# Fillers ahead of the first projection, an earlier load and narrower attention levels in a two-layer decoder trunk

## The chip, the cores and the metric

The kernel runs on one core of a Trainium2 chip. TensorE (PE) multiplies, VectorE (DVE) and ScalarE (ACT) do the elementwise work, GpSimd (POOL) does a few small operations and issues accumulating DMAs, SyncE (SP) issues the other DMAs. The metric is the device time of one execution in microseconds (us); lower is better.

## The reference

A hybrid decoder trunk of two layers over 512 positions and 1024 channels, in float32. Layer 0 mixes with an RG-LRU recurrence, layer 1 with gated linear attention; each mixer is followed by a convolutional gated FFN. Every sub-layer has an RMSNorm before and after, and adaLN gives shift, scale and gate from a conditioning vector `c`.

```python
c_act = jax.nn.silu(c)
for i in range(DEPTH):
    mod = (c_act @ ada_w[i] + ada_b[i])[:, None, :]
    sh_m, sc_m, gt_m, sh_f, sc_f, gt_f = jnp.split(mod, 6, axis=-1)
    h = rmsnorm(x, norm_g[i, 0]) * (1.0 + sc_m) + sh_m
    y = rglru_mixer(h, ...) if i % 2 == 0 else gla_mixer(h, ...)
    x = x + gt_m * rmsnorm(y, norm_g[i, 1])
    h = rmsnorm(x, norm_g[i, 2]) * (1.0 + sc_f) + sh_f
    x = x + gt_f * rmsnorm(conv_ffn(h, ...), norm_g[i, 3])
```

The first thing that TensorE has to project is `h @ rg_w_in` of layer 0, and `h` needs the row norms of `x` and the shift and scale of layer 0, so `c_act @ ada_w`. In the attention of layer 1 a chunk's decay products are formed level by level over blocks of 1, 2, 4 to 64 positions.

## The kernel before

Everything is transposed: channels lie on the 128 partitions (eight tiles `k`), positions on the 512 columns. Weights come in units of 128x1024 float32 (`unit`, loaded by `load_upto` on SP's queue into `raw`), are rounded to a single-pass type (fp32r) on ACT (`w`'s high half), and the rest is formed on DVE (low half) or, for some units, by an accumulating DMA of POOL (`accum`). Each product is three single-pass products: high x high, low activation x high, high x low weight (`mm3`). Matrix products of plain float32 need more passes; in the profile one of them leaves two records.

The kernel's operations are recorded first and then ordered by a planner (`Sched.order`, lines 190 to 344) that simulates the engines: TensorE's and SP's operations have the order of their recording as priority, and one that is not ready by the planner's clock is passed by later ones; DVE, ACT and POOL take the longest remaining chain first. The order that comes out is fixed on each engine. The planner adds 1.5 us to an accumulating DMA's end (line 325). Its clocks set the order only. On the chip each engine waits for semaphores in this order. Since helpers record every operation, all TensorE products carry line 455, DVE's lines 384, 397 and 408, ACT's 431 and 436.

The stretch that the change touches most stands at lines 519 to 671 and 882 to 913:

- SP loads `c` (`crow`), four pairs of `x`, parameters, the identity, and then row by row `adaT` tiles (`ada`) and weight units.
- TensorE spreads `c` over the partitions with two products of one row by 512 columns (`pc`), ACT applies silu to them (`cact`).
- ACT squares the eight tiles of `x`, DVE adds them in the groups of `SQ_GROUPS`. TensorE sums each group over the partitions with four 128x1 products (`nr0`), with fillers ahead of the groups by `WARM`: one four-pass product of `ones` and `x[0]` ahead of the first and of the second.
- `rstd_from` scales the sums on ACT (`sm`), raises them to -1/2 on POOL (`pow`) and spreads them with four 128x128 products (`rb0`).
- For each `k`, `ada_col` multiplies a 128x1024 tile of `adaT` by `cact` and sums the rows on DVE (once for scale, part 1; once for shift, part 0), ACT turns the sums into a column of `mod`. `h_tile` makes `t2` on DVE, the high half `hh` on ACT and the low half `hl` on DVE. Then TensorE adds 24 products into the eight accumulators `xps`. The tile `k = 0` goes in two halves of 256 columns (`FH`).

Behind it `conv4` reads the accumulators: ACT starts each with one tap, DVE adds three more (the "taps", `g<-mm,const,g`); they free the PSUM banks that the next projections (`gproj`) need. In the attention, `level_mm` multiplies, for each level `hb` and each of four blocks, up to 128 stationary columns with 64 moving ones, and `masked` copies the part that counts:

```python
        rows = P - hb
        rows = rows if rows <= 96 else P
        e.mms([(ps[t * n:(t + 1) * n].rows(rows), xt[t * P:t * P + rows], part3(xt[tsl(t)], 2 * hb, hb, 2 * hb),
```

## Time and profile before

| | us |
|---|---|
| median of 3 runs | 1181.31 |
| the runs | 1181.24, 1181.31, 1183.03 |
| the profiled execution | 1182.17 |
| its span, first to last instruction | 1180.40 |
| TensorE busy in it | 1167.3 |
| DVE, ACT, POOL busy | 839.4, 558.8, 45.5 |

Busy TensorE is modelled: matmuls are pipelined and the end of one lies behind the start of the next, so a busy share does not tell how fast products follow each other. For that, count how many start in a stretch. The granted clock is the share of full speed that the chip's record of the clock shows for a stretch; where there is no record, as ahead of the first change, the column shows 1.00. "Idle before" in brackets is the time for which an engine stood still before an instruction, and what ended it.

### The profile page before, as it was taken

Reading aid. Unit: us, or ns where it says so; the run is one execution under the profiler, and the core shown is the slowest. Engines: PE = TensorE matmul, PEld = TensorE weight load, DVE = VectorE, ACT = ScalarE, POOL = GpSimd, SP = SyncE. Lnnn points to the kernel's source line nnn. Section 1 sums busy time; section 2 is a strip of 40 time slices with the busy share of each in tenths; the row PEclk is TensorE's granted clock in tenths of the full one; section 3 lists DMA queues with packets and bytes.
Section 4 is the critical chain, followed back from the end, with each engine's and each line's share of the span. In section 5 each row is a group of like instructions: output and inputs, shape, how many; then the busy total and the mean of one; then the engine's idle time right before and its main releaser. Section 6 shows DMA issues by size and latency. Waiting matters only on the chain.

```text
span 1180.4 us, 16718 instructions
## 1 busy us (share of the span) xinstructions
PE 1167.3 (99%) x6556; PEld 1015.8 (86%) x6556; DVE 839.4 (71%) x1392; ACT 558.8 (47%) x882; POOL 45.5 (4%) x59
## 2 busy tenths in 40 slices
PE   8999999999999999999999999999999999999998
PEld 6876799988888888899988888999988888888897
DVE  5899978977778888568769576758745655645644
ACT  4489867643423424444478344445543333324421
POOL 0100014000000000000000000000000000000000
PEclk9999999999999999999999999999999999999999
DMA  9688589476574676221413102213142322232202
GB/s 348 246 260 268 177 263 286 163 231 218 171 221 176 204 237 202 89 92 55 141 63 107 55 24 84 72 40 105 42 156 90 107 101 96 91 106 90 72 1 72
DMA packets 48304, 165.81 MB, mean 140 GB/s; under 512 B 5249, under 2 KB 7809, under 8 KB 48226
## 3 DMA queue, kind: packets, MB, share of 16 engines
q1 hardware_dynamic: 45058, 156.36, 38.9%
q0 software_dynamic: 3168, 8.39, 3.8%
q8 instruction: 51, 0.84, 0.3%
q14 instruction: 27, 0.22, 0.1%
HBM read 162.63 MB, written 2.10 MB: 140 GB/s over the span
## 4 chain that ended last, share of the span: by engine, by line
PE 92%; ACT 3%; DVE 2%; issue 1%; DMA 1%; POOL 1%; DVEq 0%; POOLq 0%; ACTq 0%
PE mm L455 89%; PE nr L455 3%; ACT g L431 1%; DMA raw<-in_wall_dram 1%; POOL sm L388 1%; ACT w L436 1%; DVE gh L384 1%; ACT L431 1%; DVE g L384 0%; DVE gh L397 0%; DVE w L384 0%; DVE const L384 0%; ACT w L431 0%; DMA araw<-in_c_dram 0%; DVE araw L397 0%
## 5 line engine op out<-in xcount | busy, mean ns | idle before, releaser
L455 PE MATMUL mm<-g,w 128*128 128x512 f32 (+2 forms) x5069 | 949.8, 348 | 1.8 <-ACT g L431 1.3
L455 PEld LDWEIGHTS mm<-g,w 128*128 128x128 f32 (+1 forms) x5069 | 816.9, 189 | 121.9 <-ACT g L431 2.3
L436 ACT CAST w<-raw 128x1024 fp32r<-128x1024 f32 x178 | 186.0, 1046 | 213.7 <-PE mm L455 202.7
L384 DVE TENSOR_TENSOR w<-raw,w 128x1024 fp32r<-128x1024 f32 (+1 forms) x168 | 203.6, 1216 | 84.8 <-ACT w L436 83.9
L397 DVE SCALAR_TENSOR_TENSOR g<-mm,const,g 128x510 f32<-128x510 f32 (+3 forms) x205 | 151.0, 747 | 106.7 <-ACT g L431 96.2
L384 DVE TENSOR_TENSOR g<-g,g 128x512 f32<-128x512 f32 (+2 forms) x199 | 117.7, 613 | 35.0 <-ACT g L431 27.0
L431 ACT ACTIVATE g<-mm,const 128x512 f32<-128x512 f32 (+1 forms) x147 | 101.4, 696 | 18.6 <-PE mm L455 18.6
L455 PE MATMUL mm<-g,g 128*128 128x256 f32 (+4 forms) x748 | 103.1, 293 | 0.0
L431 ACT ACTIVATE g<-g 128x512 f32<-128x512 f32 (+1 forms) x132 | 66.5, 539 | 74.4 <-DVE g L397 65.9
L455 PEld LDWEIGHTS mm<-g,g 128*128 128x128 f32 (+1 forms) x748 | 95.2, 191 | 4.2
L397 DVE SCALAR_TENSOR_TENSOR araw<-araw,const 128x1024 f32<-128x1024 f32 x72 | 86.5, 1220 | 4.7 <-DMA araw<-in_adaT_dram 4.6
L436 ACT CAST g<-g 128x512 fp32r<-128x512 f32 (+1 forms) x63 | 39.1, 623 | 104.1 <-DVE g L384 103.2
L384 DVE TENSOR_TENSOR g<-g,mm 128x512 f32<-128x512 f32 (+1 forms) x80 | 45.2, 579 | 41.2 <-PE mm L455 40.6
L384 DVE TENSOR_TENSOR gh<-gh,gh 128x256 f32<-128x256 f32 x97 | 40.8, 422 | 25.3 <-ACT gh L431 23.4
L388 POOL TENSOR_TENSOR sm<-sm,const 128x2 f32<-128x2 f32 (+1 forms) x19 | 20.4, 1073 | 917.0 <-DVE sm L408 901.0
L455 PE MATMUL mm<-w,g 128*128 128x512 f32 x192 | 46.2, 394 | 0.0
L455 PEld LDWEIGHTS mm<-w,g 128*128 128x128 f32 x192 | 35.4, 188 | 7.0
L431 ACT ACTIVATE gh<-g 128x256 f32<-128x256 f32 x32 | 13.1, 416 | 54.8 <-DVE g L384 54.8
L431 ACT ACTIVATE g<-gh,const 128x256 fp32r<-128x256 f32 x50 | 23.6, 504 | 24.1 <-DVE gh L397 23.5
L436 ACT COPY g<-mm 128x512 f32<-128x512 f32 (+1 forms) x36 | 19.7, 560 | 24.6 <-PE mm L455 24.6
L397 DVE SCALAR_TENSOR_TENSOR w<-w,const 128x1024 f32<-128x1024 f32 x24 | 28.9, 1220 | 1.0 <-DMA w<-in_adaT_dram 1.0
L431 ACT ACT_TABLE_LOAD x22 | 28.2, 1283 | 1.1 <-PEq L1312 0.7
(72 smaller groups left out, 536.9 us busy)
## 6 DMA issues: line engine op xcount, KB each, us to landing
raw<-in_wall_dram SPq DMA_DIRECT2D x192, 512.0 KB, 3.6
araw<-in_adaT_dram SPq DMA_DIRECT2D x72, 512.0 KB, 4.5
w<-in_adaT_dram SPq DMA_DIRECT2D x24, 512.0 KB, 8.4
w<-in_wall_dram POOLq DMA_DIRECT2D x10, 512.0 KB, 8.5
g<-in_wall_dram POOLq DMA_DIRECT2D x12, 256.0 KB, 9.8
const<-in_xT_dram SPq DMA_DIRECT2D x4, 512.0 KB, 5.4
out_dram<-const SPq DMA_DIRECT2D x8, 256.0 KB, 2.3
araw<-in_masks_dram SPq DMA_DIRECT2D x1, 512.0 KB, 4.9
```

Source lines behind the costliest of these rows:

```text
L384: self.s.add(eng, dur, lambda: e.tensor_tensor(out.ap(), a.ap(), b.ap(), op=op), [a, b], [out])
L388: lambda: self.nc.gpsimd.tensor_tensor(out.ap(), a.ap(), b.ap(), op=ALU.pow), [a, b], [out])
L397: return self.nc.vector.scalar_tensor_tensor(out.ap(), a.ap(), f(sc), b.ap(), op0=op0, op1=op1, **kw)
L431: return self.nc.scalar.activation(out.ap(), a.ap(), func, **kw)
L436: self.s.add("act", (0.095 if self._sb(a) else 0.052) + out.n * 0.8325e-3, lambda: self.nc.scalar.copy(out.ap(), a.ap()), [a], [out])
L455: r.append(self.nc.tensor.matmul(g[0].ap(), g[1].ap(), g[2].ap(), start=g[3], stop=g[4], **kw))
```

## The change

Five edits. (1) The two four-pass fillers go. In their place stand single-pass products of 512 columns, `idle(j)`, which multiply a rounded copy of `ones` (`onesr`, made by ACT) by one of its columns spread over 512, into the last accumulator `xps[6]`: 3 recorded ahead of the `pc` products, 12, 1, 1 and 1 ahead of the four groups of sums, 6 ahead of `rstd_from`'s spreading and 5 behind it. The accumulators are made early, and `pc` uses two of them. (2) For `k = 0` the shift's `adaT` tile is recorded, and so loaded, ahead of the weight unit. (3) For `k = 0` (`quick`) `hh` is made by DVE's tensor_scalar instead of ACT. (4) The planner takes an accumulating DMA to end 3.5 us instead of 1.5 us after its transfer. (5) Levels whose `rows` are over 96 use `P - hb` stationary columns instead of 128.

```diff
-                    o.end = dma_free + 1.5
+                    o.end = dma_free + 3.5
...
-WARM = (1, 1, 0, 0)
+WARM = (3, 12, 1, 1, 1, 6, 5)
...
+    xps = [mmtile() for m in range(MMB)]
+
+    onesr = const(P, FR)
+    e.acopy(onesr[:], ones[:])
+
+    def idle(j):
+        for _ in range(WARM[j]):
+            e.mms([(xps[MMB - 1][:], onesr[:], onesr[0:1].map(lambda a: a.to_broadcast([P, S]), S), True, True)])
+
+    idle(0)
     for i in range(2):
-        pc = mmtile()
+        pc = xps[i]
...
-        for _ in range(WARM[j]):
-
-            e.mms([(idle[:], ones[:], x[0], True, True)])
+        idle(1 + j)
...
+    idle(5)
     rb0 = rstd_from(nr0, NT, D, True)
+    idle(6)
...
-        e.act(hh[sl], t2, AF.Identity, bias=sh)
+        if quick:
+            e.ts(hh[sl], t2, sh, None, ALU.add)
+        else:
+            e.act(hh[sl], t2, AF.Identity, bias=sh)
...
-    xps = [mmtile() if m < MMB else s.buf("nr") for m in range(NX)]
+    xps.append(s.buf("nr"))
...
         ada_col(1, k)
+        if k == 0:
+            ada_col(0, k)
         w = unit("rgx", k)
-        ada_col(0, k)
+        if k:
+            ada_col(0, k)
         for sl in parts:
-            h_tile(h, k, sl, (rs0 if k else rb0)[sl], sl.stop - sl.start, 0, 0)
+            h_tile(h, k, sl, (rs0 if k else rb0)[sl], sl.stop - sl.start, 0, 0, k < FH)
...
         rows = P - hb
-        rows = rows if rows <= 96 else P
```

TensorE from its first product to the first projection, before. `araw_84` is `crow`, `const_82` is `ones`, `nr_149` holds the sums and then their spread, `g_126` to `g_159` are the groups of squares, `g_201` and `g_204` are the halves of `h`, `w_179` is the first weight unit.

```order
L455 MATMUL mm_122<-araw_84,const_82 128x512
L455 MATMUL mm_124<-araw_84,const_82 128x512
L455 MATMUL mm_135<-const_86,const_82 128x512 x2
L455 MATMUL nr_149<-const_82,g_126 128x1 x4
L455 MATMUL nr_149<-const_82,g_145 128x1 x4
L455 MATMUL nr_149<-const_82,g_155 128x1 x4
L455 MATMUL nr_149<-const_82,g_159 128x1 x4
L455 MATMUL nr_149<-const_97,sm_184 128x128 x4
L455 MATMUL mm_209<-g_201,w_179 128x256
```

The same stretch of TensorE, after. `const_101` is `onesr`, `mm_121` the accumulator that takes the fillers.

```order
L455 MATMUL mm_121<-const_101 128x512 x5
L455 MATMUL mm_130<-araw_84,const_82 128x512
L455 MATMUL mm_134<-araw_84,const_82 128x512
L455 MATMUL mm_121<-const_101 128x512 x10
L455 MATMUL nr_167<-const_82,g_132 128x1 x4
L455 MATMUL mm_121<-const_101 128x512
L455 MATMUL nr_167<-const_82,g_154 128x1 x4
...
L455 MATMUL nr_167<-const_82,g_174 128x1 x4
L455 MATMUL mm_121<-const_101 128x512 x9
L455 MATMUL nr_167<-const_97,sm_206 128x128 x4
L455 MATMUL mm_121<-const_101 128x512 x2
L455 MATMUL mm_130<-g_231,w_208 128x256
```

Two of the twelve fillers recorded ahead of the first group have moved ahead of the `crow` products, and three of the five recorded behind the spreading stand ahead of it.

DVE around the first tile of `h`, before. `w_103`, `w_107`, `w_109` and `w_113` are `adaT` tiles (each row is a row sum), `const_130` is `cact`, `const_175` the columns of `mod`, `gh_197` and `gh_199` are `t2`.

```order
L397 SCALAR_TENSOR_TENSOR w_103,const_169<-w_103,const_130 128x1024
L384 TENSOR_TENSOR w_179<-raw_105,w_179 128x1024
L397 SCALAR_TENSOR_TENSOR w_107,const_169<-w_107,const_130 128x1024
L397 SCALAR_TENSOR_TENSOR w_109,const_169<-w_109,const_130 128x1024
L397 SCALAR_TENSOR_TENSOR gh_197<-const_86,const_175,nr_149 128x256
L397 SCALAR_TENSOR_TENSOR gh_199<-const_86,const_175,nr_149 128x256
L397 SCALAR_TENSOR_TENSOR g_204<-gh_197,const_175,g_201 128x256
L397 SCALAR_TENSOR_TENSOR w_113,const_169<-w_113,const_130 128x1024
L397 SCALAR_TENSOR_TENSOR g_204<-gh_199,const_175,g_201 128x256
```

The same stretch of DVE, after. `w_103`, `w_105`, `w_109` and `w_115` are the `adaT` tiles, `w_208` is the first unit, `gh_224` and `gh_235` are `t2`, `g_231` is `hh`, `g_233` is `hl`.

```order
L397 SCALAR_TENSOR_TENSOR w_103,const_181<-w_103,const_138 128x1024
L397 SCALAR_TENSOR_TENSOR w_105,const_181<-w_105,const_138 128x1024
L384 TENSOR_TENSOR w_208<-raw_107,w_208 128x1024
L397 SCALAR_TENSOR_TENSOR gh_224<-const_86,const_188,nr_167 128x256
L408 TENSOR_SCALAR g_231<-gh_224,const_188 128x256
L397 SCALAR_TENSOR_TENSOR g_233<-gh_224,const_188,g_231 128x256
L397 SCALAR_TENSOR_TENSOR gh_235<-const_86,const_188,nr_167 128x256
L397 SCALAR_TENSOR_TENSOR w_109,const_181<-w_109,const_138 128x1024
L408 TENSOR_SCALAR g_231<-gh_235,const_188 128x256
L397 SCALAR_TENSOR_TENSOR w_115,const_181<-w_115,const_138 128x1024
L397 SCALAR_TENSOR_TENSOR g_233<-gh_235,const_188,g_231 128x256
```

Two row sums stand ahead of the first `t2` instead of three, the making of `hh` has come over from ACT, and two row sums stand between the parts of the second half. The small steps that prepare the recurrence's lambda (128x8), which stood in the third tile of `h` with a wait for POOL's `pow`, now stand partly behind the third tile and, with the wait, behind the eighth.

ACT from the last squares to the first casts, before: `g_159` is the last square, `w_179` the first unit's cast, `sm_181` the scaled sums.

```order
L431 ACTIVATE g_159<-const_86 128x512
L431 ACTIVATE const_175<-const_169,const_157,const_95 128x1
L436 CAST w_179<-raw_105 128x1024
L431 ACTIVATE sm_181<-nr_149,const_90 128x4
L431 ACTIVATE const_175<-const_169,const_95 128x1
L436 CAST w_195<-raw_111 128x1024
```

ACT at the same place, after: `w_208` is the first unit's cast, `sm_199` the scaled sums.

```order
L431 ACTIVATE g_174<-const_86 128x512
L431 ACTIVATE const_188<-const_181,const_172,const_95 128x1
L431 ACTIVATE sm_199<-nr_167,const_90 128x4
L431 ACTIVATE const_188<-const_181,const_95 128x1
L436 CAST w_208<-raw_107 128x1024
L436 COPY g_226<-nr_167 128x512
```

The first unit's cast has moved behind the scaled sums. At ACT's very start a table load and the copy that makes `onesr` now stand ahead of the table load for silu. Elsewhere POOL's order is the same, SP's differs by two exchanged neighbours, and TensorE's by a few exchanged triples of products in the first FFN.

## Rows read from the trace of the kernel before

**Rows 1.** The page, busy time of each engine and share of the span.

```profile
PE 1167.3 (99%) x6556; PEld 1015.8 (86%) x6556; DVE 839.4 (71%) x1392; ACT 558.8 (47%) x882; POOL 45.5 (4%) x59
```

**Rows 2.** Waits of PE, whole span: us in total, times, longest.

```profile
PE nr L455 <- POOL sm L388: 2.4, 3, 1.8
```

**Rows 3.** Timeline to 60 us, PE: start, us, instructions, idle before and its releaser.

```profile
2.43 3.75 PE L455 MATMUL mm<-araw,const 1*128 1x512 f32 x4 [2.43 <-DMA araw<-in_c_dram]
...
6.11 3.78 PE L455 MATMUL mm<-const,const 128*128 128x512 f32 x4
...
9.69 6.83 PE L455 MATMUL nr<-const,g 128*128 128x1 f32 x32
...
18.27 2.08 PE L455 MATMUL nr<-const,sm 128*128 128x128 f32 x8 [1.76 <-POOL sm L388]
...
21.60 5.16 PE L455 MATMUL mm<-g,w 128*128 128x256 f32 x21 [1.26 <-ACT g L431]
...
22.12 4.34 PEld L455 LDWEIGHTS mm<-g,w 128*128 128x128 f32 x20 [0.23 <-DVE g L397]
```

**Rows 4.** Windows, PE alone: length, busy us (instructions), granted clock, DMA share, GB/s.

```profile
22.12:24.12 2.00, 2.00 (x10) 1.00 1.02 406
...
27.32:28.52 1.20, 1.20 (x10) 1.00 0.91 358
...
30.41:35.88 5.47, 5.47 (x27) 1.00 0.67 261
```

**Rows 5.** Windows, last 2 us: PE, PEld, DVE, ACT, POOL busy; clock; DMA.

```profile
1178.25:1180.40 2.15, 0.00 (x0) 0.00 (x0) 0.00 (x0) 0.00 (x0) 0.00 (x0) 0.50 0.24 85
```

**Rows 6.** Groups by form, whole span: four-pass products of 512 columns; busy us, mean ns.

```profile
L455 PE MATMUL mm<-g,raw 128*128 128x512 f32 x48 | 21.1, 592 | 0.0
```

**Rows 7.** Timeline, PE, 650 to 665 us: column sums in the attention stage.

```profile
657.18 0.95 PE L455 MATMUL nr<-const,g 128*128 128x1 f32 x8
657.99 2.34 PE L455 MATMUL mm<-g,w 128*128 128x512 f32 x9
```

**Rows 8.** Windows, PE, PEld, DVE, ACT, POOL busy; clock; DMA.

```profile
80.00:110.00 30.00, 30.00 (x118) 21.85 (x117) 29.73 (x48) 29.15 (x39) 1.75 (x2) 1.00 0.90 279
110.00:140.00 30.00, 29.72 (x121) 21.75 (x119) 27.42 (x42) 29.88 (x43) 1.75 (x2) 1.00 0.70 221
```

**Rows 9.** Timeline to 60 us, ACT, POOL and DVE up to the first `h`.

```profile
0.74 1.28 ACT L431 ACT_TABLE_LOAD   x1 [0.74 <-PEq L1312]
...
16.61 0.26 ACT L431 ACTIVATE sm<-nr,const 128x4 f32<-128x4 f32 x1 [2.80 <-PE nr L455]
...
17.02 1.20 POOL L388 TENSOR_TENSOR sm<-sm,const 128x4 f32<-128x4 f32 x1 [15.96 <-ACT sm L431]
...
20.47 0.87 DVE L397 SCALAR_TENSOR_TENSOR gh<-const,const,nr 128x256 f32<-128x256 f32 x2 [3.11 <-PE nr L455]
```

**Rows 10.** DVE groups by form, whole span: nearest to `quick`.

```profile
L408 DVE TENSOR_SCALAR g<-g,sm 128x128 f32<-128x128 f32 x12 | 2.8, 279 | 0.1
```

**Rows 11.** DVE groups by form, 20 to 64 us: row sums, low half of a 256-column tile.

```profile
L397 DVE SCALAR_TENSOR_TENSOR w<-w,const 128x1024 f32<-128x1024 f32 x13 | 15.6, 1220 | 0.0
...
L397 DVE SCALAR_TENSOR_TENSOR g<-gh,const,g 128x256 fp32r<-128x256 f32 x2 | 1.0, 482 | 0.2 <-ACT g L431 0.2
```

**Rows 12.** Timeline, DVE and ACT, 30 to 73 us: the waits.

```profile
32.18 0.17 DVE L408 TENSOR_SCALAR const<-const 128x8 f32<-128x8 f32 x1 [1.53 <-POOL const L388]
...
46.95 1.05 ACT L436 CAST w<-raw 128x1024 fp32r<-128x1024 f32 x1 [2.71 <-PE nr L455]
...
48.99 0.75 DVE L397 SCALAR_TENSOR_TENSOR g<-g,const,g 128x512 fp32r<-128x512 f32 x1 [2.04 <-ACT g L431]
...
64.77 7.99 DVE L397 SCALAR_TENSOR_TENSOR g<-mm,const,g 128x511 f32<-128x511 f32 x12 [0.56 <-ACT g L431]
```

**Rows 13.** Timeline, PE, 560 to 680 us: levels with 128 and 96 columns.

```profile
627.43 1.00 PE L455 MATMUL mm<-g 128*128 128x64 f32 x8
...
641.02 0.81 PE L455 MATMUL mm<-g 128*96 128x64 f32 x8
```

More of the change, by code (lines that the diff above doesn't have):

```diff
@@ L651, in trunk @@
     e.act(warm[:], ones[0:1], AF.Silu, table="silu")
+    xps = [mmtile() for m in range(MMB)]
[5 more added lines that the diff above has]
+    idle(0)
     for i in range(2):
-        pc = mmtile()
+        pc = xps[i]
         e.mms([(pc[:], ones[0:P].rows(1), crow[i * S:(i + 1) * S].rows(1), True, True)])
         e.act(cact[i * S:(i + 1) * S], pc[:], AF.Silu, table="silu")
-    nr0, idle = s.buf("nr"), mmtile()
+    nr0 = s.buf("nr")
     sums0 = []
@@ L713, in new_h, with h_tile @@
         return [(gt(FR), gt(FR)) for _ in range(KD)]
-    def h_tile(h, k, sl, rb, n, layer, part_sh):
+    def h_tile(h, k, sl, rb, n, layer, part_sh, quick=False):
         t2 = gtn(n)
```

## The prediction

> **What bounds the kernel now.** I read the page's busy table first: TensorE is busy 1167 us of 1180 [rows 1]. Since its matmul ends are modelled, I looked next at who makes it wait: its longest entry, waits on POOL, comes to 2.4 us, of which 1.8 in one piece [rows 2]. So there is little idle time to remove, and the one long piece lies before the first projection. Third, TensorE's own timeline of the first 36 us [rows 3]: products with `crow` (2.43), two four-pass filler products (6.11), 32 column sums (9.69 to 16.52), the broadcast of the row scales (18.27), the first projection from 21.60, with its weight loads in a row from 22.12, after a last wait for DVE. The second tile of `h` follows at 30.41 [rows 4]. Fourth, spacing: ten 128x256 products in 2.00 us at 22 to 24 us, ten in 1.20 at 27.3 to 28.5 [rows 4]. The granted clock reads 1.00 there and 0.50 only in the last 2 us [rows 4, 5], but it cannot be read so early: 512 columns in two passes take about 0.9 us a record at 6.11 (four in 3.78), 48 records of the same form took 21.1 us later, 0.44 each [rows 3, 6]. [...] Ahead of the rise stand 5.5 us of unbroken single-pass products; 7.3 us of one-row and four-pass products from 2.43 on did not bring it, nor did 6.8 us of column sums. The low rate costs the sums 0.21 us a record (6.83/32); at the high one eight stand in 0.81, from 657.18 to the next row at 657.99: 0.10 [rows 3, 7].
>
> Fifth, what follows: from 80 to 140 us DVE and ACT are busy nearly throughout, 57 and 59 us of 60 [rows 8]. An earlier TensorE is worth something there only if they are earlier too.
>
> **The change, part by part.** The profiled execution took 1182.17 us (span 1180.40), 0.86 above the median of the three runs, 1181.31; the sum is made against 1182.17.
>
> *Up to the end of the sums.* TensorE now issues 5 fillers, the two `crow` products, 10 fillers, and a filler between the groups of sums. The start stays at 2.4: the copy `onesr` stands behind a table load that ended at 2.03 anyway, and the second table load (1.28) fits in before ACT's first square, which waits for `x` [rows 9]. A single-pass filler of 512 columns costs twice a 256 one: 0.43 at the low rate (2.00/10 to 5.16/21, doubled, is 0.40 to 0.49), and 0.23 at the high rate (5.47/24) [rows 3, 4]. So 2.4 + 5 x 0.43 + 3.7 + 10 x 0.43 = 12.55. The sums at the high rate: 32 x 0.10 + 3 x 0.23 = 3.9, end 16.45, against 16.52 now. What the sums gain is thus spent on the fillers ahead of them, unless the clock rises within the ten: each second at the high rate saves half, so 0 to 2.1 us; no row decides, and I take 0.6, nearer the late end because 5.5 us went before the one rise that the trace has. End 15.85.
>
> *Sums to first h tile.* Now 1.75 us pass over ACT (0.26) and POOL (1.20), then 2.2 to DVE's start at 20.47 [rows 3, 9]. Nine fillers (9 x 0.23 = 2.05) lie in that shadow and stick out by 0.3. The eight broadcast records take 0.9 at the high rate, eight sums' 0.81 and a little for their 128 columns, and 0.4 of handover: DVE starts at 15.85 + 2.05 + 1.3 = 19.2, 1.3 earlier. Unit 0's cast now stands behind the statistics on ACT (0.26, then a short column of `mod`, then 1.05 as the cast in [rows 12]), and DVE's subtraction, as long as a row sum (1.22 [rows 11]), behind it: ready some 2.8 us after the sums, hidden behind the 3.3 above.
>
> *`quick`.* The h tile's high half moves from ACT to DVE, two handovers less; from DVE's start to TensorE's it takes 1.13 us now (20.47 to 21.60). The nearest row for the new instruction is TENSOR_SCALAR 128x128 at 279 ns, the upper bound the 482 of a 128x256 tile [rows 10, 11]; I take 0.33. TensorE gets both halves about 1.3 us after DVE's start, at 20.5 against 22.12. DVE's second half of tile 0 now has two row sums (1.22 each) between its parts [rows 11]: about 0.5 us of waiting. 48 x 0.12 + 0.5 = 6.3, so the second tile starts at 26.8 against 30.41: TensorE alone is 3.6 us ahead.
>
> *`adaT` ahead of the weights.* Both are 128x1024 on one queue, so the last of tile 0's three arrives when it did. The order decides only that DVE does two row sums before the sums end instead of three: one (1.15) moves behind.
>
> *DVE from there to the convolution taps* (20.47 to 64.77, 44.3 us). Removed: 1.53 waiting for POOL (the lambda steps move behind the last h tile), 0.56 at the taps, and about 1.0 of the 2.04 at 48.99, which goes back to ACT's cast at 46.95 and that to a weight slot that TensorE frees [rows 12]. Added: 1.15 and 2 x 0.33. Net 1.3 less. With the 1.3 above this makes 2.6; some of what is removed will come back as other waits, so I take 2.5. TensorE waits there for PSUM banks that the taps free, so DVE's figure counts, not 3.6. From 64.77 the same instructions follow in the same order on DVE and ACT: 2.5 is carried on.
>
> *Later POOL landings in the planner (1.5 to 3.5).* It exchanges some triples of products of the first feed-forward layer. TensorE's waits of that stage are in [rows 2] already, so nothing is to gain; cost 0, bounds -0.3 to +0.3.
>
> *Attention levels.* The stationary columns of five levels fall from 128 to 127, 126, 124, 120 and 112, 31 columns in all, in eight records each and four heads. Eight records took 1.00 us at 128 and 0.81 at 96 [rows 13], 0.19 per 32 columns, so 31 columns in four heads give 4 x 0.19 x 31/32 = 0.74. I take 0.7; bounds 0 (another engine may be late there) and 0.9.
>
> Sum: 2.5 + 0.7 = 3.2 less: 1182.17 - 3.2 = 1179.0 us.
>
> [...] The trace shows the clock low through 7.3 us of products that are not single-pass [rows 3]. [...]
>
> **The rivals.** *The clock does not rise before the sums (slower).* Ten single-pass products make 4.3 us without a break, less than the 5.5 that stood ahead of the one rise in the trace. Then every filler is paid at 0.43: sums end 12.55 + 6.83 + 1.3 = 20.7; nine fillers 3.9 against a shadow of 1.75; broadcast 2.2: DVE starts at 26.8, 6.3 later. The 1.3 and 0.7 come off: 1182.17 + 4.3 = 1186.5. It decides from the point where the rise misses the first group of sums. Against it: fillers stand ahead of and behind `crow` too, 10 us without a gap.
>
> *It rises and falls again during the sums.* At the end of the kernel the granted clock is 0.50 from 1178.25 on, when no product runs any more [rows 5]; among the sums only a filler in each 0.8 us keeps the array streaming. Nine fillers at 0.43 and a broadcast of 2.2 put DVE at 15.85 + 3.9 + 2.2 = 22.0, 1.5 later; 1.3 and 0.7 come off: 1182.17 - 0.5 = 1181.7. [...]
>
> *DVE is no limit.* If its waits fall further than I took, TensorE's 3.6 passes whole: 1182.17 - 4.3 = 1177.9, 1176.4 with an early rise. For it: DVE's waits at 32.18 and 48.99 come to 3.6 us [rows 12]. Against it: [rows 8].
>
> **How the numbers follow.** 0.2% of 1181.31 is 2.4 us, about what a measurement of this kernel can tell from no change; faster means below 1178.95. Forecast 0.57, its own range 1177.3 to 1180.4 (the rise between the ten fillers' first and last, the waits): half of it faster, 0.29 and 0.28. TensorE's gain whole: 0.13 (0.12 faster, 0.01 same). Falls again: 0.11 (0.10 same, 0.01 slower). Never up in time: 0.19 (0.17 slower, 0.02 same). Faster 0.41, same 0.41, slower 0.18. The range goes from 1176.0, below the third rival's early rise, to 1184.0, which takes in the second rival and the milder part of the first; the rest of the first, 0.15, and a little below are left out.
>
> **What would show it.** Right: the column sums 0.10 apart, not 0.21; DVE's first h tile near 19.2 us and the second tile's products near 26.8; the taps near 62.3, with TensorE waiting a little between 62 and 70; attention records a few ns closer. Wrong: sums at 0.21 and a first projection after 26 us (first rival); sums at 0.10 and broadcast at 0.21 (second); taps before 61 us (third). A fall in time with sums at 0.21 would refute the whole account of the clock, and so would taps that come as late as now with a time that falls by over 2 us.

## The result and the profile after: slower by 0.45%

The changed kernel takes 1186.36 us (median of 6 runs, 1185.89 to 1188.67), the kernel before 1181.48 beside it (6 runs, 1178.98 to 1183.03): a ratio of 1.0045, 95% interval 1.0031 to 1.0058. The forecast was 1179.0, its range ended at 1184.0. The profiled execution took 1186.09 us, its span 1184.0. One run of the kernel before, beside e13 to e15, was in a slow state (5799 us); it is left out of the ratios and of every count below.

The page of the changed kernel, busy time of each engine (before: [rows 1]):

```profile
PE 1169.8 (99%) x6581; PEld 1016.6 (86%) x6581; DVE 840.3 (71%) x1394; ACT 560.0 (47%) x882; POOL 44.8 (4%) x59
```

TensorE's timeline of the changed kernel up to the second tile (before: [rows 3, 4]); columns are start, us, instructions:

```profile
2.38 2.50 PE L455 MATMUL mm<-const 128*128 128x512 f32 x5 [2.38 <-ACT const L436]
...
8.52 4.19 PE L455 MATMUL mm<-const 128*128 128x512 f32 x10
12.55 0.95 PE L455 MATMUL nr<-const,g 128*128 128x1 f32 x8
...
16.19 1.71 PE L455 MATMUL nr<-const,g 128*128 128x1 f32 x8
17.76 4.19 PE L455 MATMUL mm<-const 128*128 128x512 f32 x9
21.74 1.35 PE L455 MATMUL nr<-const,sm 128*128 128x128 f32 x8
...
24.15 3.09 PE L455 MATMUL mm<-g,w 128*128 128x256 f32 x21 [0.62 <-DVE g L408]
...
30.77 4.95 PE L455 MATMUL mm<-g,w 128*128 128x512 f32 x21
```

Windows of the same stretch, cut where the granted clock changes: length, busy us (instructions), clock (1.00 in the first row stands for "no record yet"; from 22.35 on it stays at 1.00 up to the kernel's last us), DMA share, GB/s:

```profile
8.52:12.11 3.59, 3.59 (x10) 1.00 1.03 417
12.11:15.52 3.41, 3.41 (x29) 1.00 1.03 419
15.52:22.35 6.83, 6.83 (x23) 0.50 1.03 406
```

The eight sums at 12.55 take 0.95, the eight at 16.19 take 1.71: the clock rose at 12.11, near the end of the ten fillers, and fell at 15.52, among the sums. So nearly all of the ten fillers and all nine behind the sums ran at the low rate. DVE's first `t2` and, further on, its taps (before: [rows 9, 12]):

```profile
23.13 0.48 DVE L397 SCALAR_TENSOR_TENSOR gh<-const,const,nr 128x256 f32<-128x256 f32 x1 [2.50 <-PE nr L455]
```

```profile
66.58 7.98 DVE L397 SCALAR_TENSOR_TENSOR g<-mm,const,g 128x511 f32<-128x511 f32 x12 [0.56 <-ACT g L431]
```

DVE starts 2.66 later than before and reaches the taps 1.81 later. TensorE's second tile is only 0.36 later (30.77 against 30.41), yet from the taps on its products are 1.7 later, as DVE's are, which fits DVE setting the pace there. A second loss, which no term of the prediction had, stands at the end of the RG-LRU's output projection. ACT and TensorE of the changed kernel, 170 to 190 us:

```profile
182.69 0.63 ACT L431 ACTIVATE g<-raw 128x512 fp32r<-128x512 f32 x1 [2.21 <-DMA raw<-in_wall_dram]
```

```profile
181.09 0.58 PE L455 MATMUL nr<-const,gh 128*128 128x1 f32 x4 [1.24 <-DVE gh L384]
185.82 0.71 PE L455 MATMUL nr<-const,sm 128*128 128x128 f32 x4 [1.53 <-POOL sm L388]
```

ACT waits for a weight load (`raw`), DVE for ACT, the row scales of the projection for DVE, TensorE for these. The load and the accumulating DMA that POOL issues beside it, in the changed kernel (SP's queue, then POOL):

```profile
170.99 0.38 SPq L461 DMA_DIRECT2D raw<-in_wall_dram  x1
```

```profile
169.95 0.91 POOL L466 DMA_DIRECT2D w<-in_wall_dram  x1
```

and in the kernel before, with ACT's use of that load:

```profile
169.54 0.43 SPq L461 DMA_DIRECT2D raw<-in_wall_dram  x1
```

```profile
169.62 0.89 POOL L466 DMA_DIRECT2D w<-in_wall_dram  x1
```

```profile
177.91 0.62 ACT L431 ACTIVATE g<-raw 128x512 fp32r<-128x512 f32 x1
```

Before, the load is issued 0.08 us ahead of POOL's transfer and ACT takes it 8.4 us later without waiting. In the changed kernel it is issued 1.04 behind, and is there only after 11.7.

What stands just ahead of POOL's transfer decides the order: POOL's power (`pow`) for the row scales of the projection (`sm`), and beside it a row sum of DVE over an `adaT` tile (`araw`). Before:

```profile
168.03 1.62 POOL L388 TENSOR_TENSOR sm<-sm,const 128x2 f32<-128x2 f32 x1 [0.57 <-DVE sm L408]
```

```profile
167.86 1.22 DVE L397 SCALAR_TENSOR_TENSOR araw<-araw,const 128x1024 f32<-128x1024 f32 x1
```

In the changed kernel:

```profile
169.16 0.71 POOL L388 TENSOR_TENSOR sm<-sm,const 128x2 f32<-128x2 f32 x1 [0.57 <-DVE sm L408]
```

```profile
169.30 1.23 DVE L397 SCALAR_TENSOR_TENSOR araw<-araw,const 128x1024 f32<-128x1024 f32 x1 [0.22 <-DMA araw<-in_adaT_dram]
```

Where the row sum is already running when the power starts, the power takes 1.62 and POOL's transfer comes out behind SP's load. In the changed kernel DVE waited 0.22 for its tile, the power started first and took 0.71, and POOL's transfer came out ahead. All 17 profiles divide in this way: the power takes 1.62 to 1.72 in the ten in which the row sum runs, 0.71 in the seven in which it still waits for its tile. In the eleven without fills on POOL (e4, below) the order of the two transfers goes with it: seven times the load is 0.08 ahead, four times POOL's transfer by 1.04 to 1.14.

The attention levels of the changed kernel, TensorE (before: [rows 13], eight records of 128 columns 1.00):

```profile
624.21 1.88 PE L455 MATMUL mm<-g 128*127 128x64 f32 x16
631.45 0.97 PE L455 MATMUL mm<-g 128*124 128x64 f32 x8
```

The table gives, for every kernel that ran, the start of the same instruction in its profile less that in the profile of the kernel before: DVE's first `t2` (20.47 before), its first tap (64.77), and TensorE's products that stand at 160, 195 and 816 us before. Median and ratio (to the kernel before run beside it) are of the timed runs.

| kernel | t2 | taps | 160 | 195 | 816 | median us | ratio, 95% |
|---|---|---|---|---|---|---|---|
| the change | 2.66 | 1.81 | 1.71 | 4.08 | 3.53 | 1186.36 | 1.0045, 1.0031 to 1.0058 |
| e1_plan15 | 3.23 | 2.50 | 2.39 | 5.39 | 4.85 | 1185.80 | 1.0037, 1.0025 to 1.0050 |
| e2_nofill | -0.43 | -1.06 | -1.16 | -0.50 | -1.02 | 1181.69 | 1.0003, 0.9991 to 1.0014 |
| e3_levels | -2.41 | -3.57 | -3.63 | -3.28 | -3.80 | 1178.69 | 0.9981, 0.9969 to 0.9994 |
| e4_poollate | 3.04 | 2.10 | 2.00 | 0.92 | 0.38 | 1183.50 | 1.0022, 1.0011 to 1.0033 |
| e5_dense | 8.82 | 7.79 | 7.70 | 7.14 | 7.11 | 1184.83 | 1.0039, 1.0020 to 1.0057 |
| e6_nolate | 1.11 | 1.40 | 1.28 | 1.13 | 0.76 | 1182.38 | 1.0019, 1.0005 to 1.0033 |
| e7_best | -1.66 | -0.22 | -0.35 | -0.84 | -1.37 | 1180.67 | 1.0000, 0.9986 to 1.0014 |
| e8_best0 | -1.67 | -2.43 | -2.52 | 0.26 | -0.28 | 1180.72 | 0.9999, 0.9987 to 1.0011 |
| e9_levels_pad | -0.19 | -0.72 | -0.82 | -0.71 | -1.23 | 1179.73 | 0.9992, 0.9980 to 1.0003 |
| e10_start | -3.08 | -2.95 | -3.05 | -2.74 | -3.29 | 1178.24 | 0.9982, 0.9974 to 0.9991 |
| e11_start0 | -2.99 | -0.97 | -1.10 | -1.43 | -1.97 | 1178.05 | 0.9979, 0.9970 to 0.9988 |
| e12_before_nofill | -0.27 | -0.44 | -0.52 | 2.64 | 2.65 | 1183.22 | 1.0025, 1.0015 to 1.0035 |
| e13_long | 9.53 | 8.46 | 8.35 | 8.33 | 8.13 | 1187.48 | 1.0072, 1.0049 to 1.0095 |
| e14_long_dense | 7.68 | 7.26 | 7.14 | 11.49 | 10.96 | 1188.59 | 1.0057, 1.0032 to 1.0083 |
| e15_start9 | -3.11 | -2.94 | -3.06 | -1.92 | -2.45 | 1177.89 | 0.9986, 0.9974 to 0.9998 |

The five columns of shifts are of one execution, and the executions of one kernel differ (e3 below), so a sign at one place is not yet an effect of the edit.

### The profile page after: what moved, and what is told of

It reads as the page before. It is cut to its first block, busy times and chain, and to the rows that moved or that the text cites. A ratio compares the mean times of both kernels' runs of the same rounds, so it can differ in the third digit from the quotient of the medians.

```text
span 1184.0 us, 16769 instructions
## 1 busy us (share of the span) xinstructions
PE 1169.8 (99%) x6581; PEld 1016.6 (86%) x6581; DVE 840.3 (71%) x1394; ACT 560.0 (47%) x882; POOL 44.8 (4%) x59
## 4 chain that ended last, share of the span: by engine, by line
PE 86%; DVE 5%; ACT 4%; DMA 3%; issue 2%; POOL 0%; DVEq 0%; SPq 0%; POOLq 0%; ACTq 0%
PE mm L455 85%; DMA raw<-in_wall_dram 2%; PE nr L455 2%; ACT g L431 2%; DVE w L397 1%; DVE w L384 1%; DVE g L397 1%; ACT w L436 1%; DVE gh L384 1%; POOL sm L388 0%; ACT L431 0%; DMA araw<-in_adaT_dram 0%; DVE gh L397 0%; ACT w L431 0%; DVE araw L397 0%
```

## The experiments

The theory from the two profiles: 1.7 us come from the fall of the clock, which puts DVE late; 2.3 from the two transfers at 170 us. The rivals: the planner's edit, or the moved row sums and the high half on DVE.

### Does the planner's edit cost anything? (e1)

```diff
-                    o.end = dma_free + 3.5
+                    o.end = dma_free + 1.5
```

> The changed kernel with one edit undone: the planner's allowance for an accumulating DMA is 1.5 us again, which puts 26 rows of TensorE's order (triples of products of the first feed-forward layer) elsewhere and leaves the orders of DVE, ACT, POOL and SP as they are. My theory (the changed kernel lost 1.7 us up to the convolution taps, because the clock fell among the sums, and 2.3 us at 180 to 184 us, because a weight load of SP came behind an accumulating DMA of POOL): the time stays within 0.5 us of the changed kernel's, since the loss at 180 us lies ahead of those products; TensorE still waits some 1.4 us near 179.6 and 1.7 us near 184.0. Rival (the planner's edit costs what was lost between 141 and 190 us): 2.3 us faster than the changed kernel and both waits gone.

Measured: 1185.80, 0.56 below the changed kernel, where up to 0.5 was expected, with ratios whose intervals overlap almost wholly. The loss between 160 and 195 us is there again (2.39 to 5.39). The planner's edit is not the cause.

### Do the fillers cost it? (e2, e6, e12)

e2 leaves out all fillers of the changed kernel, e6 the eleven behind the sums, e12 the two four-pass ones of the kernel before:

```diff
-WARM = (3, 12, 1, 1, 1, 6, 5)
+WARM = (0, 0, 0, 0, 0, 0, 0)     # e2
+WARM = (3, 12, 1, 1, 1, 0, 0)    # e6
...
-WARM = (1, 1, 0, 0)
+WARM = (0, 0, 0, 0)              # e12, kernel before
```

> The changed kernel without any filler (all seven counts zero); everything else of the change stays. My theory: the sums run at the low rate, 0.21 us a record, but each group starts as soon as its squares are there (8.6, 10.1, then the next ones), so they end near 15.4 us; DVE's first h tile (t2) starts near 19.3 us against 23.1 in the changed kernel and 20.5 in the kernel before, and the taps start near 62.3 against 66.4. Time: 4 us less than the changed kernel, and, if the weight load at 170 us comes ahead of the accumulating DMA again, 6 us less: 1180 to 1182, at or a little below the kernel before. Rival (the fillers are not what costs; the moved row sums, the high half on DVE or the load order are): taps within 0.7 us of the changed kernel's and a time above 1184.

> The changed kernel without the eleven fillers behind the column sums (nine ahead of the spreading of the row scales, two behind it). If those fillers, at the low rate (4.0 us), are what puts DVE late: the spreading starts as soon as POOL's power is there, near 19.5, and takes 2.1; t2 near 21.8 instead of 23.1; 1.2 us less at 79 us, and 1.2 less in the whole time at the same order of transfers at 170 us. Rival (they lie in the shadow of ACT and POOL, and the late sums are the whole cause): t2 within 0.3 of 23.1.

> The kernel before without its two four-pass fillers and nothing else changed (all orders are the same). The account in the prediction (four-pass and one-row products do not raise the clock; the fillers cost a little time): the sums start near 8.9 instead of 9.69, and the time falls by 0.5 to 0.9 us. Rival (they do raise it in those executions in which the chip looks at the right moment, as at 9.07 us in e3; about a third of the executions of the kernel before show a mean granted clock of 0.994 to 0.996 and are 2 to 3 us faster): without them no execution is below 1179.5 and none has a mean granted clock below 0.998, while the slower ones are 0.5 to 0.9 faster.

e2: 1181.69, 4.7 less than the changed kernel and within the expected 1180 to 1182. Its sums, and DVE's first `t2`:

```profile
8.75 6.99 PE L455 MATMUL nr<-const,g 128*128 128x1 f32 x32 [2.65 <-DVE g L384]
```

```profile
20.04 0.48 DVE L397 SCALAR_TENSOR_TENSOR gh<-const,const,nr 128x256 f32<-128x256 f32 x1 [1.57 <-ACT g L436]
```

The sums end at 15.7 even at the low rate. `t2` comes at 20.04 and misses the expected 19.3, since ACT's copy of the row scales now stands ahead of it and DVE waits for that copy; the taps come at 63.71 instead of 62.3.

e6: the spreading starts at 19.47, `t2` at 21.58, 1.55 earlier than in the changed kernel (expected 1.3):

```profile
19.47 2.07 PE L455 MATMUL nr<-const,sm 128*128 128x128 f32 x8 [1.58 <-POOL sm L388]
```

So the nine fillers stuck out of their shadow by about that much. The median fell by 4.0, not by 1.2: the loss at 170 us is gone too (1.28 to 1.13), though nothing was changed there. POOL's power and transfer in e6:

```profile
169.15 1.63 POOL L388 TENSOR_TENSOR sm<-sm,const 128x2 f32<-128x2 f32 x1 [0.57 <-DVE sm L408]
170.75 0.89 POOL L466 DMA_DIRECT2D w<-in_wall_dram  x1
```

The power starts within 0.01 us of where it starts in the changed kernel (169.16), but DVE's row sum is running, and SP's load is out first (170.66). So being some us later is not what exchanged the two transfers.

e12 refutes the prediction's account of the four-pass fillers. The sums start at 8.78 instead of 9.69, but the kernel is 0.25% slower than before, and none of its 12 runs is below 1181.28. What the fillers bring is told by the mean granted clock that is listed for each run. In 118 runs of the kernel before, made beside the kernels here, 59 have a mean of 0.996 or less and a median of 1179.2, and 59 have more and a median of 1182.0. In e12 no run has 0.996 or less. That such a mean goes with an early rise and a fall after it is what e3 shows, in one profile. The clock is not all of e12's loss, though: its median, 1183.2, is 1.2 above that of the 59 runs without an early rise, and its profile loses 3.2 us between 160 and 195 us.

### The narrower attention alone, and a second draw of the kernel before (e3, e9)

```diff
-        rows = rows if rows <= 96 else P
```

> The kernel before with the narrower attention levels alone. From the changed kernel's trace, where an offset of 4.05 us ahead of the attention became 3.5 behind it: 0.5 to 0.7 us faster than the kernel before, with no record earlier than 600 us moved by more than 0.2. Rival (in the attention another engine sets the pace, so that narrower products only wait): within 0.2 us of the kernel before.

Up to 600 us e3 is the kernel before, instruction for instruction. Yet its profiled execution is 3.6 us ahead at 30 us. Its sums, and windows cut where its clock changes:

```profile
9.31 4.34 PE L455 MATMUL nr<-const,g 128*128 128x1 f32 x32
```

```profile
5.96:9.07 3.11, 3.11 (x5) 1.00 1.00 379
9.07:12.49 3.42, 3.36 (x29) 1.00 1.03 419
12.49:22.73 10.24, 6.77 (x29) 0.50 1.03 409
```

Here the clock rose at 9.07, behind the `crow` products and the four-pass fillers, in the same code in which it rose only at 27.96 in the profile of the kernel before. The sums took 4.34 instead of 6.83, and DVE started 2.41 earlier. The low stretch that follows, 10.24 us at half the clock, is what a mean of 0.996 over some 1,170 us amounts to. So, by the mean clock, half of the executions of the kernel before have the early rise, and the one whose profile the prediction was made from had not. Nine of e3's 12 runs had it, so its median, 2.6 below that of the kernel before beside it, is mostly that draw. Like with like, it is 0.6 with the early rise (1178.6 against 1179.2) and 0.4 without (1181.5 against 1182.0, three runs). In every profile with the edit, TensorE gains 0.5 between 570 and 816 us, unless another wait takes it (e5, e13). That is the expected 0.5 to 0.7; the expectation that nothing would move ahead of it was wrong.

e9 adds six fills of a spare tile on POOL ahead of the accumulating DMA (the helper is shown with e4):

> The kernel before with the narrower attention levels and with six small fills of a spare tile on POOL ahead of the accumulating DMA at 169.6 us (24 of them took 6.2 us in e4, so 1.6 us). Theory: part of the slow executions of the kernel before come from SP's weight load falling behind that DMA (0.08 us ahead of it in the profile); with the fills none does, so the executions above some 1182 us go, and the attention gives 0.5: median 1179.5 to 1180.7, largest below 1182. Rival (the slow executions have another cause): the median falls by 0.5 alone and the largest stays near 1183 to 1184.

The median is level with the kernel before in that set, 1179.73 against 1179.71 (a set in which 20 of 35 runs of the kernel before had the early rise), and the interval holds a gain of 0.5. Like with like the gain is there: 1178.4 against 1179.1 in the six runs with the early rise, 1181.2 against 1181.7 in the six without. The largest of its 12 runs is 1181.58. Of the 118 of the kernel before 16 are above 1182.5, so 12 runs without one are no proof: whether those 16 come from the two transfers stays open.

### The two transfers at 170 us (e4, e8)

```diff
+        def fn():
+            r = [self.nc.gpsimd.memset(pad.ap(), 0.0) for _ in range(24 if pad is not None else 0)]
+            return r + [self.nc.gpsimd.dma_start(out.ap(), src, accum_op=ALU.add)]
...
-                e.accum(w[D:D + n], wall[j, :, :n], P * n * 4)
+                e.accum(w[D:D + n], wall[j, :, :n], P * n * 4, pool_pad if UNITS[j][0] == ("up", 0, 0) else None)
```

> The changed kernel with 24 small fills of a spare tile on POOL (24 x 0.08 = 1.9 us) ahead of one accumulating DMA, that of the first feed-forward unit, issued at 169.95 us in the changed kernel; it then goes out near 171.9, behind SP's weight load at 170.99, as it did in the kernel before (169.62 against 169.54). All other orders are the same. My theory: that load lands some 5 us after its issue instead of 11.6, ACT no longer waits 2.2 us for it at 182.7, TensorE's waits of 1.4 and 1.7 us near 180 and 184 go, and the kernel is 1.8 to 2.5 us faster than the changed one, at about 1184. Rival (the transfers there are bound by bandwidth, the order does not matter): within 0.4 us of the changed kernel, and the same wait for another transfer.

POOL in e4, and ACT's use of the load:

```profile
169.83 6.24 POOL L467 MEMSET const<- 128x128 f32 x24
176.36 1.80 POOL L468 DMA_DIRECT2D w<-in_wall_dram  x2 [0.29 <-ACT g L431]
```

```profile
179.02 0.61 ACT L431 ACTIVATE g<-raw 128x512 fp32r<-128x512 f32 x1
```

The fills took 6.2 us rather than 1.9 (the 0.08 each came from a row of four fills of different sizes). With POOL's transfer out of the way ACT does not wait, TensorE's two waits near 181 and 186 us are gone, and the shift against the kernel before goes down (2.00 at 160 us, 0.92 at 195) instead of up (1.71, 4.08). The median falls by 2.9, a little more than expected. Nothing but POOL differs, so the second loss of the changed kernel is this collision. What the DMA engines moved from 172 to 178 us (TensorE alone; clock, DMA share, GB/s), in the changed kernel and in e4:

```profile
172.00:178.00 6.00, 6.00 (x52) 1.00 0.90 222
```

```profile
172.00:178.00 6.00, 6.00 (x53) 1.00 0.89 345
```

At the same busy share the engines moved a third less while the accumulating transfer ran.

e8 is e7 (below) without the fills.

> The kernel of e7 without the fills on POOL. The orders of all other engines are the same. Theory of the two transfers at 170 us: the start is that of e7; where SP's weight load is issued ahead of POOL's accumulating DMA the time is that of e7 within 0.4, and where it is issued behind it 2.5 to 3.5 us more, with ACT waiting for the load near 180. Rival (the order does not matter in this phase): as e7 whatever the order.

In its profile POOL's transfer is ahead (165.61 against 166.75) and the loss is there, from -2.52 at 160 us to 0.26 at 195. ACT and TensorE:

```profile
178.87 0.63 ACT L431 ACTIVATE g<-raw 128x512 fp32r<-128x512 f32 x1 [3.88 <-DMA raw<-in_wall_dram]
```

```profile
182.00 0.71 PE L455 MATMUL nr<-const,sm 128*128 128x128 f32 x4 [3.19 <-POOL sm L388]
```

By the medians, though, e7 and e8 are equal, so how often e8 loses this way is not shown. The landings in the traces (the updates of the load's own semaphore) show the order over all 17 profiles: in the four in which POOL's transfer is 1.04 to 1.14 ahead (the change, e1, e8, e14) the load lands 11.7 to 12.1 us after its issue, and in twelve of the thirteen others after 4.4 to 7.3. The exception is e12, where the load is ahead by 0.08 (169.68 against 169.76), as before, and ACT still waits for it:

```profile
181.25 0.63 ACT L431 ACTIVATE g<-raw 128x512 fp32r<-128x512 f32 x1 [2.28 <-DMA raw<-in_wall_dram]
```

There 15 of the load's 16 parts land after at most 6.6 us and the last one after 11.6. A lead of 0.08 us was enough in six profiles and not in this one.

### Why does the clock fall among the sums? (e5, e13, e14)

e5 has four fillers instead of one between the groups of sums. e13 has three times the fillers ahead of the sums and one between; e14 is e13 with four between. The planner's counts are untouched:

```diff
-            e.mms([(xps[MMB - 1][:], onesr[:], ..., True, True)])
+            e.mms([(xps[MMB - 1][:], onesr[:], ..., True, True)],
+                  rep=4 if j in (2, 3, 4) else 1)              # e5
+                  rep={1: 3, 2: 1, 3: 1, 4: 1}.get(j, 1))      # e13
+                  rep={1: 3, 2: 4, 3: 4, 4: 4}.get(j, 1))      # e14
```

> The changed kernel with four fillers instead of one between the groups of column sums (nine more in all; the planner counts them as before, so that all other orders are the same). The theory that the clock fell because the sums alone left TensorE too thinly occupied: from its rise at 12 to 14 us the granted clock stays at the upper level, the 32 sums stand 0.10 apart throughout and end near 18.5 us (12.55 + 3.24 + 12 x 0.22), the nine fillers behind them take 2.05 instead of 4.0, and DVE's first t2 starts near 21.9, 1.2 earlier than in the changed kernel. Rival (the clock falls whatever stands between the sums): the last sums and the nine fillers at the low rate again, t2 after 24.5. The whole time follows by the same 1.2, plus or minus some 3 us by the order of the two transfers at 170 us; so the place at 79 us is the measure.

e5 tells nothing on that question: in its profiled execution the clock did not rise until 27.63, so every filler and sum up to there was paid at the low rate and `t2` came at 29.29. This is the prediction's first rival. One group and its fillers:

```profile
16.36 1.71 PE L455 MATMUL nr<-const,g 128*128 128x1 f32 x8
17.93 2.05 PE L455 MATMUL mm<-const 128*128 128x512 f32 x4
```

It does show that 25 us of products in a row (2.38 to 27.63: fillers, the `crow` products, sums and fillers by turns) may pass before the rise.

> The changed kernel with three times the fillers ahead of the column sums (9 ahead of the products with c instead of 5 by the planner's order, 30 behind them instead of 10), so that the clock rises before the sums in every execution; one filler between the groups of sums, as in the changed kernel. If the sums with one filler between them are what lets the clock fall: granted clock 1.0 from 9 to 14 us on, the first group of sums at 0.10 a record, then 0.50 within 7 us of the first sum, and the late sums or the nine fillers at the low rate. Rival (in the changed kernel the clock fell because it had only just risen; after a long run of fillers it stays): no fall before the first projection. The time itself says little: some 4 us of fillers are added.

> The kernel of e13 with four fillers instead of one between the groups of sums; all other orders are the same. If it is the thin occupation by one-column products that lets the clock fall: no fall before the first projection, 32 sums at 0.10, nine fillers in 2.1 us, spreading at the high rate; t2 1.5 to 2 us earlier than in e13, although nine fillers (1.9 us) more stand ahead of it. Rival (four fillers do not hold it either): a fall as in e13, and t2 1.9 us or more later.

e13, windows cut where the clock changes, and its last group of sums:

```profile
15.43:22.26 6.83, 6.83 (x44) 1.00 1.03 405
22.26:29.08 6.82, 6.82 (x23) 0.50 0.40 132
```

```profile
23.18 1.71 PE L455 MATMUL nr<-const,g 128*128 128x1 f32 x8
24.75 4.19 PE L455 MATMUL mm<-const 128*128 128x512 f32 x9
```

e14, its last group and the fillers behind it:

```profile
24.20 0.95 PE L455 MATMUL nr<-const,g 128*128 128x1 f32 x8
25.01 2.21 PE L455 MATMUL mm<-const 128*128 128x512 f32 x9
```

With one filler the clock fell again, although it had been up for some 4 us of unbroken fillers ahead of the sums. With four it held from 14.39 to 191.89, and `t2` came 1.85 earlier than in e13, as expected, although nine fillers more stand ahead of it. So with a single filler between them the sums let the clock fall, in all five profiles in which it rose ahead of them (the change, e1, e4, e6, e13); that four hold it rests on the one profile of e14. Against e13 the nine fillers save more than they cost. With the 24 more that stand ahead of the sums in both, `t2` is still 5.0 later than in the changed kernel, so no kernel here gains by them; whether four fillers would pay behind the ten of the change is not shown, since e5's profile had no rise.

### What would a better start be worth? (e7, e10, e11, e15)

The sums' place in the chain suggests fewer of them. e7: two groups of squares, so 16 records instead of 32, fewer fillers, and e4's fills. e10: also the fillers forced behind the `crow` products, ACT's copy behind both `t2`, six fills. e11 has no filler, e15 nine.

```diff
-SQ_GROUPS = ((0, 1, 2, 3), (4, 5), (6,), (7,))
-WARM = (3, 12, 1, 1, 1, 6, 5)
+SQ_GROUPS = ((0, 1, 2, 3), (4, 5, 6, 7))
+WARM = (0, 5, 0, 0, 0, 4, 0)     # e7, e8
+WARM = (0, 5, 0, 0, 0, 0, 0)     # e10; e11: 0, e15: 9 instead of 5
...
-    e.acopy(rs0[:], rb0[:])
+        if k == 0:
+            s.add("act", 0.5, lambda: nc.scalar.copy(rs0[:].ap(), rb0[:].ap()), [rb0[:]], [rs0[:]], after=(t2op,))   # e10, e11, e15
```

> The changed kernel with three changes: the squares are summed in two groups (tiles 0 to 3 and 4 to 7) instead of four, which halves TensorE's column sums from 32 to 16 records and adds two 0.69 us additions on DVE; fillers only where TensorE would stand still (five between the products with c and the first sums, four behind the last sums); and the accumulating DMA at 170 us delayed by fills on POOL as in e4. Theory (sums at the low rate on TensorE set DVE's start): first sums 8.75 to 10.5, second from about 11.1 to 12.9, spreading at 14.5 to 16.6, t2 near 16.8 against 20.5 in the kernel before; the taps 3.7 to 4.4 us earlier than before; 0.5 of it goes at 165 us; with 0.5 from the attention 1176.5 to 1178 in all. Rival (a load or DVE's row sums are next late): t2 or the taps no more than 2 us earlier than before, and a time of 1179 or more.

e7 missed: `t2` at 18.81, since the order put five fillers ahead of `crow` and ACT's copy ahead of `t2`, and in its profile the taps are only 0.22 ahead, held by a weight load for which ACT waits 6.89 us at 62.79.

> The changed kernel with: squares in two groups; five fillers only, made to come behind the two products with c and in the gap ahead of the first sums; ACT's copy of the row scales behind the two t2 of the first tile (in e2 and e7 it stood ahead of them and DVE waited 1.4 to 1.6 us for it); six fills on POOL ahead of the accumulating DMA at 170 us. Theory (the sums at the low rate, and what stands ahead of them, set DVE's start): first sums 8.7 to 10.5, second 11.8 to 13.5, t2 near 17.4 against 20.5 before, 18.8 in e7 and 23.1 in the changed kernel; the taps 2 to 3 us earlier than in the kernel before; time 1177.5 to 1179.5. Rival (the weight load that ACT awaits at 60 us sets the taps, not DVE): t2 as said, taps less than 1.5 us earlier and a time above 1179.5.

e10, TensorE's sums and DVE's `t2`:

```profile
9.00 1.86 PE L455 MATMUL nr<-const,g 128*128 128x1 f32 x8 [0.40 <-DVE g L384]
11.84 1.86 PE L455 MATMUL nr<-const,g 128*128 128x1 f32 x8 [0.97 <-DVE g L384]
```

```profile
17.39 0.48 DVE L397 SCALAR_TENSOR_TENSOR gh<-const,const,nr 128x256 f32<-128x256 f32 x1 [0.80 <-PE nr L455]
```

`t2` at 17.39, the taps 2.95 earlier than before, 1178.24 us: as expected, below the kernel before (0.9982, 0.9974 to 0.9991) and 8.1 below the changed kernel. This has no high clock at all ahead of the first projection.

> The kernel of e10 without its five fillers; the orders are the same otherwise. Theory (fillers that stand in a gap can only help, by raising the clock early in some executions): t2 the same to 0.3 us in executions without an early rise; the first rise of the clock never before 20 us; the median 0 to 1 us above e10's. Rival (fillers do nothing at all here, or hold up the sums): the median at or below e10's.

> The kernel of e10 with nine fillers instead of five behind the products with c (3.9 us instead of 2.2 at the low rate; the first sums 1.0 later, at 10 us, the second group at 11.8 as before). If a longer unbroken run of fillers ahead of the sums brings the early rise in more executions: t2 0 to 0.4 later than in e10 without a rise, 1 to 1.5 earlier with one; the median 0.3 to 1 us below e10's 1178.24. Rival (TensorE has not been occupied long enough by then): no rise before 20 us and a median within 0.4 of e10's.

e11 and e15 are level with e10 (1178.05 and 1177.89); e11 was expected 0 to 1 above it and is 0.2 below. Nine fillers do bring an early rise, by the mean clock in 5 of 10 runs, where five bring it in none of 12; the time does not follow (1178.2 with it, 1177.4 without). In e11's profile the weight load at 62 us is late again and costs 2:

```profile
62.04 1.06 ACT L431 ACTIVATE w<-raw 128x1024 fp32r<-128x1024 f32 x1 [6.89 <-DMA raw<-in_wall_dram]
```

## Why the prediction was wrong

It was wrong in sign and outside its range, by 7.1 us on the profiled execution (1179.0 against 1186.09). That the time is close to the 1186.5 of its first rival is chance: that rival has no rise before the sums, and here the clock rose. By its own steps:

- **Fillers and sums, end at 15.85.** This step failed: it took all sums at the high rate. The clock fell at 15.52, and the last sums stretched the end to 17.76. 1.9 lost. The sums began at 12.55, which is the figure worked out without any saving, but two errors cancel there: the first five fillers took 2.43 (2.15 worked out), and the ten 4.03, which is 0.4 less than the 4.43 that they take wholly at the low rate in e5. So the rise at 12.11 saved 0.4 of the 0.6 taken. The 0.6 leans on 5.5 us of unbroken single-pass products ahead of the one rise; no run shows that a rise takes them. By the clock's record 5.84 stood ahead of it in the profile of the kernel before (22.12 to 27.96), 3.59 here (8.52 to 12.11), none in e3 (9.07).
- **Sums to `t2`, 3.35.** This failed with it: nine fillers at the low rate took 4.0 (2.05 taken) and the spreading began in the low stretch: 5.4 from 17.76 to 23.13. 2.0 lost. Together this is the second rival, "rises and falls again", which had a chance of 0.11, a start of DVE at 22.0 and a time of 1181.7. Its price was short because it left the end of the sums at 15.85 and had no loss behind the taps. It happened in four of the five profiles that share this start (the change, e1, e4, e6; not e5).
- **`quick` and the load order.** The new instruction takes 0.35 (0.33 taken). From `t2` to the taps 0.85 less was spent, 1.3 forecast. The direction is right. A weight load that ACT awaits ahead of the taps takes part of it: in the changed kernel ACT waits 5.38 for it until 64.82. Edits 2 to 5 together are worth about 1.5 by the medians of e2 and e12 (1181.69, 1183.22), neither of which has fillers; 0.5 of it is the attention's, and part of the rest may be the collision at 170 us, which e12's profile has and e2's has not.
- **"2.5 is carried on."** This step failed outright. The instructions that follow are indeed the same, but not the transfers' place among each other. SP's load came out 1.04 behind POOL's transfer instead of 0.08 ahead of it, which cost 2.3 us at 180 us in the profile and 2.9 in the median (e4). No rival had it. By the profiles, what exchanged them is DVE's wait of 0.22 for an `adaT` tile and not the delay itself (e6); no run changes that wait alone, and why the tile was late in some executions stays open. The thin margin could have been seen in the trace of the kernel before: 0.08 us between two issues, and a busy share of the DMA engines of 1.06 behind them (windows of that trace: PE, PEld, DVE, ACT, POOL busy; clock; DMA share; GB/s):

```profile
175.00:180.00 5.00, 5.00 (x44) 5.00 (x43) 4.60 (x15) 3.87 (x11) 2.05 (x3) 1.00 1.06 272
```

- **The planner's edit at 0** held (e1). **The attention at 0.7** was 0.5.

The sum of the misses: 1.9 + 2.0 + 0.4 to the taps, 2.3 at the transfers, 0.2 in the attention and 0.3 behind them, most of it outside the span, make 7.1.

The root of the first two is how the clock was read from one execution. That execution shows one rise and no fall before the kernel's end, so the sum took the clock to stay up once it had risen. A second execution of the same code, e3's, has the rise at 9.07 and the fall among the sums at 12.49. From the same execution the prediction concluded that 7.3 us of one-row and four-pass products "did not bring" the rise. e3's rise at 9.07, behind just such products, and e12, in which without the four-pass ones no run has a mean of 0.996 or less, speak against that. The two executions of the same code have the rise 18.9 us apart (9.07 and 27.96), and the 118 runs divide into two halves of 59, so one trace could not carry a "never". Within a profile the changes of the clock listed here stand 3.41 us or a whole multiple of it apart (3.41 and 6.83 in the change, 3.42 and 10.24 in e3, 6.83 and 6.82 in e13); 18.9 is no such multiple, so from one execution to the other the places of the changes shifted against the kernel's start. The change thus took out fillers that raise the clock ahead of the sums in half of the executions, and put in longer ones that raise it 3 us later, at 12.11. In both the clock falls again, but in the change nine fillers then stand in the low stretch.

## What to carry to other kernels

The rise of the clock stood at 9.07 and at 27.96 us in two executions of the same code: one profile shows one draw, so look at the spread of the runs and their mean clocks before reading a rule from it. A filler cost 0.44 us ahead of the rise (ten in 4.43, e5) and 0.25 behind it (nine in 2.21, e14), and eight one-column sums between single fillers gave the rise back, within 3.4 us of it in the change and 6.8 in e13. Leaving all fillers out gave 4.7 us (e2, whose profile has no collision either), and taking work out of the chain (half the sums, a copy put behind its rival for a buffer) brought another 3.6 by the medians of e11 and e2, part of which may be e11's fills on POOL. By the profiles a wait of 0.22 us exchanged two transfers on different queues, and that cost 2.3 us, 2.9 in the median (e4): look for issues within a few tenths of each other where the busy share of the DMA engines is near 1 (1.06 here), and for what holds each of them back.

## What the runs showed of the hardware

- A product of plain float32 with 512 columns, the "four-pass" one, left two records and took 1.89 us ahead of the rise (two in 3.78, [rows 3]) and 0.88 at a clock of 1.00 (48 records in 21.1, [rows 6]); a single-pass one took 0.44 (ten in 4.43, e5) and 0.25 (nine in 2.21, e14).
- With TensorE's one-column sums and a single filler between each eight the granted clock fell back to 0.50 within 3.4 (the change) and 6.8 us (e13) of its rise; with four fillers between it held, from 14.39 to 191.89 (e14).
- The clock fell in mid-kernel, too, behind short waits of TensorE. In e12, windows of TensorE around its wait of 1.31 at 167 us:

```profile
165.00:168.96 3.96, 2.65 (x23) 1.00 0.89 252
168.96:172.38 3.42, 3.42 (x18) 0.50 0.81 160
```

- e1 and e14 show the same behind waits of 1.93 and 3.22 (0.50 from 184.23 and from 191.89), so there the wait for a late transfer was followed by a stretch at the low clock. Not everywhere: e8's wait of 3.19 at 182 us left the clock at 1.00, and so did the changed kernel's of 1.24 and 1.53 at 181 and 185.8.
- A weight load of 512 KB landed 4.4 to 7.3 us after its issue where it was issued ahead of an accumulating DMA of POOL or with it (twelve profiles; in a thirteenth its last part took 11.6), and 11.7 to 12.1 where it was issued 1.04 to 1.14 behind (four). Between 171 and 173 us SP's queue moved 0.61 MB and POOL's none in the kernel before; in the changed kernel SP's moved 0.05 and POOL's 0.23, and from 173 to 181 SP's moved 1.09 and POOL's 0.95. Why 1.04 us of order cost some 5 us of landing stays open.
- The DMA engines moved 222 GB/s at a busy share of 0.90 with an accumulating transfer of POOL under way, and 345 at 0.89 without (172 to 178 us, the change and e4).
- A power of 128x2 on POOL took 0.71 us where a row sum of DVE (128x1024) had not yet begun, and 1.62 to 1.72 where one was running, at the same place in 17 profiles. Why is not shown.
- A fill of 128x128 on POOL took about 0.26 us, in rows of 6 (1.50, e10) and of 24 (6.24, e4).
